# Strassen's seven products for twenty pairs of column blocks of the gate and up projections, and the SiLU product split into high and low parts in the down projection

## The chip, the cores and the metric

The kernel runs on one core of a Trainium2 chip. The metric is the device time of one execution in microseconds; the time before is the median of three runs. A core has a matrix engine (TensorE, in the profile PE for matmuls and PEld for the loads of their stationary operand), a vector engine (VectorE, DVE), a scalar engine (ScalarE, ACT), GpSimd (POOL), and SyncE (SP), which here issues the weight loads. Each engine works through its own queue in order and waits on semaphores for the others. TensorE writes its results to PSUM, in tiles of two halves of 512 float32 columns; everything else is in SBUF.

## The reference, cut to what matters

One layer of a hybrid encoder for 512 prompt tokens and 128 sample tokens (640 rows, `T`), 1024 features, float32. Three gated branches (a recurrence, a convolution, attention into a memory) are merged and projected, and a feed forward follows:

```python
def trunk_layer(x, ...):
    z = x @ w_in
    ...
    merged = g[:, :, 0] * out_a + g[:, :, 1] * out_b + g[:, :, 2] * out_c
    x = layer_norm(DEEPNORM_ALPHA * x + merged @ w_out, ln1_g, ln1_b)
    ffn = (jax.nn.silu(x @ w_ffn_gate) * (x @ w_ffn_up)) @ w_ffn_down
    x = layer_norm(DEEPNORM_ALPHA * x + ffn, ln2_g, ln2_b)
    return x, ...
```

`w_ffn_gate` and `w_ffn_up` are 1024 x 2816, `w_ffn_down` is 2816 x 1024. The change is in the line that makes `ffn`.

## The kernel before

**Three passes.** A float32 product is made of three matmuls in a faster format (float32r): each operand is split into a high part (a copy by ScalarE into float32r) and a low part (VectorE subtracts the copy from the original), and high x high, high x low and low x high are added up in PSUM. Every operand of these matmuls has to be split first, weights too.

**Tiling.** The activations of the feed forward lie feature-major in `xh` and `xl`: eight blocks of 128 features by 640 tokens. The columns of gate and up come in 22 blocks of 128 (`KF`). One column block is one step (`x_step`, line 696): for each of the eight blocks of features, three passes over two halves of the tokens (`HT`, 320), 48 matmuls into a PSUM tile `pu`, of which there are two. What follows (`evac`, line 1481) is done for gate by ScalarE, which writes SiLU of the result into a slot, and for up by VectorE, which multiplies the slot by the result; then the product is split at once into two slots, `hT[m]`, for the down projection. Slots are 48 SBUF buffers of 640 float32 columns, handed out in turn (`s_` and numbers in the rows).

**Steps and preparation.** The program is a list of `Step`s, written out by the loop at line 1623. A step has a weight (part of a `Load`), a generator of matmuls and an `evac`. At step i the loop first has ScalarE copy the weights of step i+2 (`prep_hi`, into `wh`, three buffers), runs the step's `before`, then issues the matmuls; at the generator's first pause it lets pending streams go on (`advance`), does the `evac` of step i-1 (`flush`), and has VectorE write the low part of the weights of step i+2 (`prep_lo`, into `wl`, three buffers). Weights come in 1 MB loads of 256 columns by SP into two buffers `wr`; a load is issued when all users of the one two before have been split (`Load.take`, `pump`).

**The start and end of the feed forward.** The first three steps (blocks 0 and 1 of gate, 0 of up) form a group: their first token halves run while the norm of the last tokens is still being made. Then come block 1 of up and the other 40 blocks, gate pair and up pair in turn. The down projection (line 1549) takes token tiles 0, 1, 2 first, 22 steps of 18 matmuls of 512 columns with `hT[k]` as the stationary operand, then tiles 3 and 4. `before_down` (line 1496) starts the loads of the residual rows.

Of the kernel before, what the change touches and what calls it, by code (L numbers as in the profile page):

```python
# [20 lines left out]
HT = T // 2  # L21
# [30 lines left out]

class Engine:
    """an engine whose instructions add to an estimate of the time until which it is busy"""
# [89 lines left out]
def trunk(ctx, tc, x_prompt, x_sample, mem_prompt, state_conv_a, state_lru, state_conv_b, cache_mem_k, cache_mem_v,  # L144
# [75 lines left out]
    class Blocks:  # L220
        """two blocks of rows of a weight, in slots"""
# [8 lines left out]
    class Row:  # L230
        """a block of rows of a weight, in slots"""
# [21 lines left out]
    class Step:  # L253
        """weights (a part of a load, in two parts), products (a generator that pauses within), what follows"""

        def __init__(self, ld, part, shape, mm, evac=None, before=None, eng=V, slot=False, wait=False, now=False):
            self.ld, self.part, self.shape, self.mm, self.evac = ld, part, shape, mm, evac
            self.before = before
# [4 lines left out]
        def prep_hi(self):  # L263
# [3 lines left out]
            if self.slot:  # L267
# [4 lines left out]
                self.todo = [(hi[c], lo[c], src[c]) for c in range(2)]  # L272
            else:
# [9 lines left out]
        def prep_lo(self):  # L283
# [5 lines left out]
            self.ld.take()  # L289

# [12 lines left out]
    def advance():  # L303
        """lets the streams go on, as far as the vector and scalar engines have time for them while TensorE is busy"""
# [18 lines left out]
    def until(cond):  # L323
        """goes on with the streams, in turn, until a condition holds"""
# [38 lines left out]
    # ---------------------------------------------------------------- constants  # L363
# [22 lines left out]
    # ---------------------------------------------------------------- early loads  # L386
# [55 lines left out]
    def ln_scale(y, mv, rs):  # L442
        """rows without their mean, over their deviation, on ScalarE"""
# [20 lines left out]
    def to_xt(t, x):  # L464
        """transposes of a token tile into xh/xl columns"""
# [137 lines left out]
    def load_rows():  # L603
        """parameters and states, as rows"""
# [45 lines left out]
    def lambda_rows():  # L650
        """8 * log_sigmoid(lambda)"""
# [17 lines left out]
    # ---------------------------------------------------------------- feature-major products  # L669
# [26 lines left out]
    def x_step(ld, o, evac, group=None):  # L696
        """128 columns of a weight, times xh/xl; in a group the first half of the tokens goes first"""
# [26 lines left out]
    # order of the weight loads and the steps -------------------------------------------------  # L724
    # glu and q
# [43 lines left out]
    # ---------------------------------------------------------------- branch B: convolution, layer norm, swish  # L769
# [49 lines left out]
    def token_row(cols):  # L819
        """[128, 5] per-token values (tokens on partitions) -> [128, 640] rows on every partition, in PSUM"""  # L820
# [5 lines left out]
    def ln_b_stream():  # L826
# [32 lines left out]
        # a hundred columns, where one would do: with fewer TensorE's clock goes down  # L859
# [59 lines left out]
    def block(p, i):  # L919
        """a quarter of a PSUM tile"""  # L920
        return p[:, i // 2, (i % 2) * 256:(i % 2 + 1) * 256]

    def attn_prompt():
# [35 lines left out]
        def queries(_):  # L959
            # queries of the samples in float32: of the even ones, of the odd ones, and zeros for the others  # L960
# [69 lines left out]
    def every(x, e):  # L1030
        """the columns of the even samples or of the odd ones"""
        return x.rearrange("p (j e t) -> p j e t", e=2, t=TS)[:, :, e]

    def attn_sample():
        """A pair of samples has 32 columns of the array and 32 partitions of the results to itself; the odd one's
        products add to zeros on the even one's rows, and the other way round."""
# [3 lines left out]
        def load(to, src, h):  # L1040
            """a head's keys or values, memory rows on partitions"""
# [100 lines left out]
    # ---------------------------------------------------------------- gates and projections  # L1142
# [60 lines left out]
    # ---------------------------------------------------------------- branch A: convolution, recurrence  # L1203
# [28 lines left out]
    def lru_stream():  # L1232
# [79 lines left out]
        # states  # L1312
# [41 lines left out]
    # ---------------------------------------------------------------- step list of the first part  # L1354
# [15 lines left out]
    # ---------------------------------------------------------------- output projection, layer norm 1  # L1370
# [4 lines left out]
    def tm(p, l, w, t, first, last, cs=(0, 1)):  # L1375
        """a token tile's products with a row of blocks of a weight"""
# [297 lines left out]
```

## Time and profile before

| | |
|---|---|
| median of three runs | 1127.92 us (1127.79 to 1129.1) |
| profiled execution | span 1129.4 us; no separate time of it is listed |
| TensorE busy | 1100.2 us (97%), 7115 matmuls |
| VectorE, ScalarE, GpSimd busy | 53%, 37%, 15% of the span |
| feed forward up to the down projection | about 658 to 969.6 us of the span |
| down projection | from 969.6 us |
| granted TensorE clock, mean | 0.993 |

The span runs from the first to the last instruction. All instructions of the five engines are issued through one helper, so rows carry line L64; they are told apart by what they write and read (`pu<-xh,wh` is a matmul of the weight's high part and the activation's high part into a tile `pu`; `s` is any slot). In the chain of waits and in the timelines the first two columns are the start and the length in us, and `[a <-B]` says how long the engine sat idle and what released it. In rows of instruction groups stand the shapes, the count, busy time in us, mean ns of one, and the idle time before. In windows each engine has its busy time and count, then come the granted clock, the DMA share and GB/s.

### The profile page before, as it was taken

What the parts mean: (1) busy time and instruction counts of PE and PEld (TensorE: products, weight loads), DVE (VectorE), ACT (ScalarE), POOL (GpSimd) and SP (SyncE); (2) the same over time, 40 slices, a digit from 0 to 9 for tenths busy, and PEclk for the clock granted to TensorE, in tenths of its full rate; (3) what the DMA queues carried; (4) which work ended last, traced back from release to release, by engine and by line L of the source; (5) the groups of instructions that cost most, each with busy time, mean ns of one, the idle gap of its engine ahead of it and who ended that gap; (6) DMA issues with size and microseconds to landing.
All of it is one profiled execution on the core that took longest, in us unless ns stands there. A gap on an engine that the chain in (4) does not pass through costs nothing.

```text
span 1129.4 us, 16818 instructions
## 1 busy us (share of the span) xinstructions
PE 1100.2 (97%) x7115; PEld 1047.0 (93%) x7115; DVE 595.5 (53%) x895; ACT 420.7 (37%) x635; POOL 170.5 (15%) x185
## 2 busy tenths in 40 slices
PE   8799998989999999999999999999999999999997
PEld 7699998979999999999998899999999999888886
DVE  6929988992465665571354763222222222322675
ACT  3532554435446556862222122222222222222341
POOL 3623333646000000010001310000000000100111
PEclk9999999999999999999999999999999999999998
DMA  9632113624122222222227223222222222634481
GB/s 340 226 102 75 38 50 113 197 81 138 53 92 75 74 77 75 75 80 75 75 76 242 93 76 112 75 75 75 75 75 75 75 75 76 234 121 133 153 292 38
DMA packets 80331, 123.11 MB, mean 109 GB/s; under 512 B 4075, under 2 KB 59371, under 8 KB 80256
## 3 DMA queue, kind: packets, MB, share of 16 engines
q1 hardware_dynamic: 73168, 100.36, 27.2%
q0 software_dynamic: 7088, 21.68, 6.1%
q8 instruction: 56, 0.92, 0.3%
q14 instruction: 19, 0.16, 0.0%
HBM read 112.41 MB, written 9.61 MB: 108 GB/s over the span
## 4 chain that ended last, share of the span: by engine, by line
PE 78%; DVE 12%; ACT 4%; issue 2%; DMA 2%; POOL 1%; SPq 0%; DVEq 0%; POOLq 0%
PE pu L64 69%; DVE s L64 10%; PE pv L64 9%; ACT s L64 2%; DVE wl L64 1%; ACT L64 1%; DMA wr<-in_w_in 1%; ACT wh L64 1%; DMA s<-in_w_mem_k 0%; DMA s<-in_w_mem_v 0%; DMA s<-in_ln_in_g 0%; POOL s L516 0%; DVE xres L64 0%; POOL s L517 0%; POOL rs L439 0%
## 5 line engine op out<-in xcount | busy, mean ns | idle before, releaser
L64 PE MATMUL pu<-xh,wh 128*128 128x320 f32 x1504 | 351.4, 311 | 2.1 <-DVE s L64 1.5
L64 PE MATMUL pu<-xl,wh 128*128 128x320 f32 x1504 | 348.5, 309 | 0.0
L64 PE MATMUL pu<-xh,wl 128*128 128x320 f32 x1504 | 348.3, 309 | 0.0
L64 ACT ACTIVATE wh<-wr 128x1024 fp32r<-128x1024 f32 (+1 forms) x161 | 163.6, 1017 | 494.4 <-PE pu L64 273.4
L64 DVE TENSOR_TENSOR wl<-wr,wh 128x1024 fp32r<-128x1024 f32 (+1 forms) x148 | 173.0, 1169 | 275.5 <-ACT wh L64 275.3
L64 PEld LDWEIGHTS pu<-xh,wh 128*128 128x128 f32 x1504 | 252.3, 188 | 5.5 <-issue 2.0
L64 PEld LDWEIGHTS pu<-xl,wh 128*128 128x128 f32 x1504 | 253.3, 188 | 0.6 <-DVE xl L64 0.6
L64 PEld LDWEIGHTS pu<-xh,wl 128*128 128x128 f32 x1504 | 253.3, 188 | 0.0
L64 DVE SCALAR_TENSOR_TENSOR s<-s,pb,s 128x511 f32<-128x511 f32 (+14 forms) x240 | 128.5, 608 | 4.8 <-ACT s L64 4.8
L64 PE MATMUL pu<-wh,s 128*128 128x512 f32 (+1 forms) x396 | 116.5, 386 | 0.0
L64 DVE TENSOR_TENSOR s<-s,s 128x640 f32<-128x640 f32 (+3 forms) x116 | 85.7, 758 | 47.2 <-ACT s L64 43.6
L64 DVE TENSOR_TENSOR s<-s,pu 128x640 f32<-128x640 f32 x48 | 39.3, 819 | 131.7 <-PE pu L64 131.7
L64 PE MATMUL pu<-s,wh 128*128 128x320 f32 x512 | 96.2, 310 | 1.1 <-DVE s L64 0.9
L64 PEld LDWEIGHTS pu<-wh,s 128*128 128x128 f32 x396 | 73.2, 190 | 14.9 <-DVE s L64 0.4
L64 PEld LDWEIGHTS pu<-s,wh 128*128 128x128 f32 x512 | 80.2, 188 | 1.9 <-DVE s L64 1.5
L64 ACT ACTIVATE s<-s 128x640 fp32r<-128x640 f32 (+3 forms) x100 | 64.1, 663 | 32.3 <-DVE s L64 31.3
L64 PE MATMUL pu<-wl,s 128*128 128x512 f32 (+1 forms) x198 | 62.8, 389 | 1.5 <-POOL wl L287 0.8
L287 POOL TENSOR_TENSOR wl<-wr,wh 128x1024 fp32r<-128x1024 f32 x13 | 48.2, 3711 | 96.3 <-ACT wh L64 90.2
L64 PE MATMUL pu<-s,wl 128*128 128x320 f32 x256 | 58.3, 309 | 0.0
L64 PE MATMUL pv<-wh,s 128*128 128x512 f32 (+1 forms) x152 | 48.7, 367 | 0.3 <-DVE xres L64 0.3
L1499 POOL DMA_DIRECT2D xres<-x x5 | 2.6, 535 | 305.6 <-PE pu L64 305.6
L64 PEld LDWEIGHTS pu<-wl,s 128*128 128x128 f32 x198 | 37.4, 191 | 10.5 <-POOL wl L287 1.7
(126 smaller groups left out, 929.4 us busy)
## 6 DMA issues: line engine op xcount, KB each, us to landing
wr<-in_w_in SPq DMA_DIRECT2D x26, 1024.0 KB, 5.7
wr<-in_w_ffn_down SPq DMA_DIRECT2D x19, 1024.0 KB, 5.7
wr<-in_w_ffn_gate SPq DMA_DIRECT2D x11, 1024.0 KB, 5.4
wr<-in_w_ffn_up SPq DMA_DIRECT2D x11, 1024.0 KB, 5.3
s<-in_cache_mem_k POOLq DMA_DIRECT2D x16, 256.0 KB, 7.6
s<-in_cache_mem_v POOLq DMA_DIRECT2D x16, 256.0 KB, 6.8
wr<-in_proj_a SPq DMA_DIRECT2D x4, 1024.0 KB
wr<-in_w_out SPq DMA_DIRECT2D x4, 1024.0 KB, 5.1
```

Of the source, the lines that this page charges most:

```text
L64: return f(*a, **k)
L287: self.eng.tensor_tensor(l, x, f32(h), op=OP.subtract)
L1499: G.dma_start(r[:, t], scratch["x1"][t * 128:(t + 1) * 128, :])
```

## The change

Block columns 0 and 1 of gate and up stay as they were, except that the product of SiLU and up stays whole, in one slot. Blocks 2 to 21 are taken in ten pairs for gate and ten for up. A pair is a 2 x 2 problem: two halves of the tokens (320 each) by two halves of the features (four blocks each), times two halves of the features by two column blocks. Winograd's form of Strassen's scheme makes it of seven products in place of eight. For that

- four sums of quarters of the activations, s1 to s4, are made once and split (`sums_stream`, a stream started when block 0 of gate is done; it has to be finished before the second product of the first pair),
- four sums of quarters of each weight tile, t1 to t4, are made by VectorE in slots (`sums_1`, `sums_2`), in the third and fourth step of the pair before,
- each product is a `Step` of its own with 12 matmuls of 320 columns. The high and low parts of its weight share one buffer, alternately of `wh` and `wl`. Products m2, m7 and m3 add onto m1, m6 and m5, in the PSUM half where those lie, after they have been read,
- the results are combined by VectorE (`after`, `put`), and SiLU and the product with it are done 320 columns at a time.

The split of the SiLU product moves: `before_down` splits blocks 0 and 1, and each of the first 20 steps of the down projection splits the block two ahead. Docstrings and comments are dropped throughout.

```diff
@@ class Step
-        def __init__(self, ld, part, shape, mm, evac=None, before=None, eng=V, slot=False, wait=False, now=False):
+        def __init__(self, ld, part, shape, mm, evac=None, before=None, eng=V, slot=False, wait=False, now=False,
+                     half=None, after=None):
...
+            elif self.half is not None:
+                n = ("wh", "wl")[self.half]
+                both = view(wp.tile([128, 1024], F32R, name=n, tag=n), [128, 2, *self.shape[1:]])
+                hi, lo = both[:, 0], both[:, 1]
+                self.todo = [(hi, lo, src)]
...
             self.ld.take()
+            if self.after:
+                self.after()
@@ feed forward
+                    hT[m] = get([128, T])
+                    A.activation(c2(hT[m]), p, AF.Silu)
+                    if m == 0:
+                        stream("sums", sums_stream())
+                else:
+                    V.tensor_mul(c2(hT[m]), c2(hT[m]), p)
...
+    def sums_stream():
+        parts = {n: ([], []) for n in ("s1", "s2", "s3", "s4")}
+        for i in range(0, half, 2):
+            a = {}
+            for n, (t0, k0) in {"21": (HT, 0), "22": (HT, half), "11": (0, 0), "12": (0, half)}.items():
+                a[n] = get([128, 2, HT])
+                V.tensor_tensor(a[n], *(f32(x[:, k0 + i:k0 + i + 2, t0:t0 + HT]) for x in (xh, xl)), op=OP.add)
+                yield "v"
+            s = {}
+            for n, p, q, op in (("s1", "21", "22", OP.add), ("s2", "s1", "11", OP.subtract),
+                                ("s3", "11", "21", OP.subtract), ("s4", "12", "s2", OP.subtract)):
+                s[n] = get([128, 2, HT])
+                V.tensor_tensor(s[n], s[p] if p in s else a[p], s[q] if q in s else a[q], op=op)
+                yield "v"
+            free(*a.values())
+            for n, x in s.items():
+                hi, lo = get([128, 2, HT], F32R), get([128, 2, HT], F32R)
+                split(hi, lo, x)
...
+        def sums_1(self):
+            self.add("t3", "22", "12", OP.subtract)
+            self.add("t2", "t3", "11", OP.add)
+
+        def sums_2(self):
+            self.add("t1", "12", "11", OP.subtract)
+            self.add("t4", "t2", "21", OP.subtract)
...
+    PRODUCTS = (("m1", 0, 0, True, "11", "11"), ("m6", 0, 1, True, "s2", "t2"), ("m2", 0, 0, False, "12", "21"),
+                ("m7", 0, 1, False, "s3", "t3"), ("m5", 1, 0, True, "s1", "t1"), ("m4", 1, 1, True, "22", "t4"),
+                ("m3", 1, 0, False, "s4", "22"))
...
+        def after(n, p):
+            if n == "m1":
+                tmp["a"], tmp["b"] = get([128, 2, HT]), get([128, 2, HT])
+                copy(tmp["a"][:, 0], p)
+            elif n == "m6":
+                V.tensor_tensor(tmp["a"][:, 1], tmp["a"][:, 0], p, op=OP.add)
+            elif n == "m2":
+                put(0, 0, p, None, None)
+            elif n == "m7":
+                V.tensor_tensor(tmp["b"][:, 0], tmp["a"][:, 0], p, op=OP.add)
+            elif n == "m5":
+                put(1, 1, p, tmp["b"][:, 0], OP.add)
+            elif n == "m4":
+                put(0, 1, p, tmp["b"][:, 0], OP.subtract)
...
+            else:
+                put(1, 0, p, tmp["a"][:, 1], OP.add)
...
+                for k in range(half):
+                    P.matmul(p, hi[:, k], xhi[k], start=start and k == 0, stop=False, skip_group_check=not start)
+                    P.matmul(p, hi[:, k], xlo[k], start=False, stop=False, skip_group_check=not start)
+                yield
+                for k in range(half):
+                    P.matmul(p, lo[:, k], xhi[k], start=False, stop=k == half - 1, skip_group_check=not start)
+                yield
...
+            if i == 1:
+                before = begin
+            elif following and i == 2:
+                before = following.sums_1
+            elif following and i == 3:
+                before = following.sums_2
...
+    last_of_first = steps[-2]
+    last_of_first.before = lambda: (pairs[0][0].sums_1(), pairs[0][0].sums_2())
...
+        def put(j, c, p, x, op, which=which, m2=m2):
+            if which == "g":
...
+                h = c2(hT[m2 + j])[:, c]
+                if x is not None:
+                    V.tensor_tensor(h, x, p, op=op)
+                A.activation(h, p if x is None else h, AF.Silu)
+            else:
+                h = c2(hT[m2 + j])[:, c]
+                if x is not None:
+                    y = get([128, HT])
+                    V.tensor_tensor(y, x, p, op=op)
+                    V.tensor_tensor(h, h, y, op=OP.mult)
+                    free(y)
+                else:
+                    V.tensor_tensor(h, h, p, op=OP.mult)
...
+    def split_h(k):
+        if k < KF:
+            hi, lo = get([128, T], F32R), get([128, T], F32R)
+            split(hi, lo, hT[k])
...
     def before_down():
+        flush()
+        free(*sums)
+        for k in range(2):
+            split_h(k)
...
                 wd[k] = halves(w)
+                if len(tiles) == 3:
+                    split_h(k + 2)
```

**How it moves instructions.** TensorE, within the feed forward. Before, from a step of one column block (both token halves each time, hence x2):

```order
L64 MATMUL pu<-xh,wh 128x320 x2
L64 MATMUL pu<-xl,wh 128x320 x2
L64 MATMUL pu<-xh,wl 128x320 x2
L64 MATMUL pu<-xh,wh 128x320 x2
L64 MATMUL pu<-xl,wh 128x320 x2
```

After, the second product of the first pair, m6, and the first row of m2. Here `wl` is a buffer with both parts of t2, `s_370` and `s_388` are the high parts of s2, `s_371` and `s_389` its low parts:

```order
L64 MATMUL pu<-s_370_6712,wl 128x320
L64 MATMUL pu<-s_371_6713,wl 128x320
L64 MATMUL pu<-s_370_6712,wl 128x320
L64 MATMUL pu<-s_371_6713,wl 128x320
L64 MATMUL pu<-s_388_6766,wl 128x320
L64 MATMUL pu<-s_389_6767,wl 128x320
L64 MATMUL pu<-s_388_6766,wl 128x320
L64 MATMUL pu<-s_389_6767,wl 128x320
L64 MATMUL pu<-s_370_6712,wl 128x320 x2
L64 MATMUL pu<-s_388_6766,wl 128x320 x2
L64 MATMUL pu<-xh,wh 128x320
```

A product is 12 matmuls into one half of a PSUM tile, and m6 reads both halves of s2, of which the second is made last.

VectorE, where the feed forward begins, behind the last split of the normed activations (`xl<-pv,xh`). Before, with the low parts of weights (`wl<-wr,wh`), the products with SiLU and their splits:

```order
L64 TENSOR_TENSOR xl<-pv,xh 128x4x128 x4
L64 TENSOR_TENSOR wl<-wr,wh 128x1024 x2
L64 TENSOR_TENSOR s_354_6585<-s_354_6585,pv 128x640
L64 TENSOR_TENSOR s_357_6662<-s_354_6585,s_356_6661 128x640
L64 TENSOR_TENSOR wl<-wr,wh 128x1024
L64 TENSOR_TENSOR s_355_6617<-s_355_6617,pu 128x640
```

After, the end of the same stretch: the second half of the sums of activations, from the whole quarters (`<-xh,xl`) over s1 to s4 (`s_382` to `s_385`) to their low parts (`s_387` to `s_393`):

```order
L64 TENSOR_TENSOR s_381_6752<-xh,xl 128x640
L64 TENSOR_TENSOR s_382_6754<-s_378_6746,s_379_6748 128x640
L64 TENSOR_TENSOR s_383_6756<-s_382_6754,s_380_6750 128x640
L64 TENSOR_TENSOR s_384_6758<-s_380_6750,s_378_6746 128x640
L64 TENSOR_TENSOR s_385_6760<-s_381_6752,s_383_6756 128x640
L64 TENSOR_TENSOR s_387_6763<-s_382_6754,s_386_6762 128x640
L64 TENSOR_TENSOR s_389_6767<-s_383_6756,s_388_6766 128x640
L64 TENSOR_TENSOR s_391_6771<-s_384_6758,s_390_6770 128x640
L64 TENSOR_TENSOR s_393_6775<-s_385_6760,s_392_6774 128x640
L64 TENSOR_TENSOR wl<-s_358_6610,wl 128x512
L64 TENSOR_TENSOR s_394_6793<-wr 128x512
L64 TENSOR_TENSOR s_395_6795<-s_394_6793,wr 128x512
```

Behind the low part of the weight of up's block 1 stand 23 instructions of 640 columns and 7 of 512 ahead of the one that writes `s_389`, the last part of s2; the two splits of SiLU products that stood there are gone.

VectorE, where the down projection begins. Before, the product for block 21 of up (`s_415`), its split, and 22 low parts of weights:

```order
L64 TENSOR_TENSOR s_414_8848<-s_414_8848,pu 128x640
L64 TENSOR_TENSOR s_417_8962<-s_414_8848,s_416_8961 128x640
L64 TENSOR_TENSOR wl<-wr,wh 128x1024
L64 TENSOR_TENSOR s_415_8905<-s_415_8905,pu 128x640
L64 TENSOR_TENSOR s_419_9015<-s_415_8905,s_418_9014 128x640
L64 TENSOR_TENSOR wl<-wr,wh 128x1024 x22
```

After, from the reading of the last product (`s_557`) on:

```order
L64 TENSOR_TENSOR s_557_9383<-s_553_9281,pu 128x320
L64 TENSOR_TENSOR s_552_9228<-s_552_9228,s_557_9383 128x320
L64 TENSOR_TENSOR s_559_9387<-s_354_6585,s_558_9386 128x640
L64 TENSOR_TENSOR s_561_9391<-s_362_6630,s_560_9390 128x640
L64 TENSOR_TENSOR s_563_9404<-s_398_6825,s_562_9403 128x640
L64 TENSOR_TENSOR wl<-wr,wh 128x1024
```

The low part of the first SiLU block, `s_559`, with which the down projection's first step works, now stands behind the reading of the last product.

More of the change, by code (lines that the diff above doesn't have):

```diff
@@ new lines, in trunk, with evac @@
+    for which in ("g", "u"):
+        for m in range(2):
+            def evac(p, m=m, which=which):
+                if which == "g":
[5 more added lines that the diff above has]
+                    V.tensor_mul(c2(hT[m]), c2(hT[m]), p)
+            x_step(zload[which], m * 128, evac, group=group if len(group[1]) < 3 else None)
+    half = KD // 2
@@ new lines, in trunk @@
+    quarters = {}
+    for n, (t0, k0) in {"11": (0, 0), "12": (0, half), "21": (HT, 0), "22": (HT, half)}.items():
+        quarters[n] = tuple([x[:, k0 + k, t0:t0 + HT] for k in range(half)] for x in (xh, xl))
+    sums = []
+    def sums_stream():
[16 more added lines that the diff above has]
+                split(hi, lo, x)
+                free(x)
+                sums.extend((hi, lo))
+                for to, y in zip(parts[n], (hi, lo)):
+                    to.extend(y[:, k] for k in range(2))
+                yield 1
+        quarters.update(parts)
@@ new lines, in trunk @@
+    pairs = []
+    for m2 in range(2, KF, 2):
+        for which, w in (("g", w_ffn_gate), ("u", w_ffn_up)):
+            pairs.append((Pair(ffn_load(w, m2, 7)), which, m2))
+    last_of_first = steps[-2]
+    last_of_first.before = lambda: (pairs[0][0].sums_1(), pairs[0][0].sums_2())
+    for i, (pair, which, m2) in enumerate(pairs):
+        def put(j, c, p, x, op, which=which, m2=m2):
+            if which == "g":
+                if m2 + j not in hT:
+                    hT[m2 + j] = get([128, T])
+                h = c2(hT[m2 + j])[:, c]
[11 more added lines that the diff above has]
+                    V.tensor_tensor(h, h, p, op=OP.mult)
+        seven(pair, put, pairs[i + 1][0] if i + 1 < len(pairs) else None,
+              begin=(lambda: finish("sums")) if i == 0 else None)
```

59 lines of the change are left out of this document (41 added, 18 removed).

## The prediction

> **What bounds the kernel now.** I read the page's engine row first, then the chain that ended last in order of time, then the feed forward stage by windows.
>
> ```profile
> span 1129.4 us, 16818 instructions
> PE 1100.2 (97%) x7115; PEld 1047.0 (93%) x7115; DVE 595.5 (53%) x895; ACT 420.7 (37%) x635; POOL 170.5 (15%) x185
> ```
>
> TensorE is busy 97% of the span, VectorE 53%, ScalarE 37%. A busy share is an average over stages, so the chain has to say where TensorE ends last:
>
> ```profile
> 667.01 3.52 PE pv L64 x24
> 670.53 7.04 PE pu L64 x48
> 677.58 3.52 PE pv L64 x24
> 681.10 291.38 PE pu L64 x1980
> 972.48 1.36 PE pv L64 x6
> ```
>
> From 681.10 on the chain is TensorE alone for 291.4 us. Those 1980 matmuls are 41 steps of 48 of the feed forward and, at the end, the first 12 of the down projection (512 wide, 1.36/6 = 0.227 us each). So (291.38 - 12 x 0.227)/1968 = 0.1467 us per 320-wide matmul, 7.04 us per column block. The row at 677.58 gives the same for 24 matmuls into one half of one PSUM tile: 3.52/24 = 0.1467. Neither a step's border nor repeated writes into one half cost anything.
>
> ```profile
> 681.00:972.00 291.00, 291.00 (x1980) 290.59 (x1979) 84.37 (x85) 72.64 (x84) 1.73 (x4) 1.00 0.25 77
> PE pv L64 <- DVE xres L64: 0.3, 1, 0.3
> ```
>
> The first row (windows: PE, PEld, DVE, ACT, POOL busy, granted clock, DMA share, GB/s) says that VectorE works 84 of these 291 us and ScalarE 73, at a granted clock of 1.00. The second is TensorE's whole list of waits from 655 us to the end. The stage is bound by the number of matmuls, and the helpers have some 200 us to spare.
>
> **Matmuls removed.** Two column blocks cost 2 x 48 = 96 matmuls. As a pair they cost seven products of four blocks of rows and three passes, 84, all 320 wide; the order lists 5232 of that width for 5472 before and the same number of every other width. So 240 go: 240 x 0.1467 = **-35.2 us**. The new passes read the same weights twice running (high part times high, high times low) as before, into one half of a tile, which the row at 677.58 prices. The rule in the Trainium skill, "TensorE: Matmul & The Clock Gate", section "Back-to-back issue gap", makes a warm gap columns/2.4 + 2.5 ns, 135.8 ns for 320; by it the term would be -32.6 and the whole sum -22.7. The trace's 146.7 is what these matmuls take, and I use it.
>
> **Prices of the helpers' work.** Rows of the instruction groups by form, and of VectorE's and ScalarE's timelines:
>
> ```profile
> L64 DVE TENSOR_TENSOR wl<-wr,wh 128x1024 fp32r<-128x1024 f32 x43 | 52.6, 1222 | 105.7 <-ACT wh L64 105.7
> L64 DVE TENSOR_TENSOR s<-s,s 128x640 fp32r<-128x640 f32 x21 | 17.3, 826 | 16.9 <-ACT s L64 16.9
> L64 DVE TENSOR_TENSOR s<-s,pu 128x640 f32<-128x640 f32 x20 | 16.4, 821 | 84.2 <-PE pu L64 84.2
> L64 DVE TENSOR_TENSOR xl<-pv,xh 128x512 fp32r<-128x512 f32 x4 | 2.6, 685 | 0.3 <-ACT xh L64 0.3
> L64 ACT ACTIVATE wh<-wr 128x1024 fp32r<-128x1024 f32 x42 | 44.6, 1062 | 217.3 <-issue 107.6 <-PE pu L64 104.1 <-PE pv L64 5.6
> L64 ACT ACTIVATE s<-s 128x640 fp32r<-128x640 f32 x20 | 14.8, 740 | 0.7
> ```
>
> ```profile
> 666.41 1.29 DVE L64 TENSOR_TENSOR xl<-pv,xh 128x512 fp32r<-128x512 f32 x2 [0.26 <-ACT xh L64]
> 675.04 1.23 DVE L64 TENSOR_TENSOR wl<-wr,wh 128x1024 fp32r<-128x1024 f32 x1 [7.34 <-ACT wh L64]
> 689.80 0.83 DVE L64 TENSOR_TENSOR s<-s,s 128x640 fp32r<-128x640 f32 x1 [0.81 <-ACT s L64]
> 690.54 1.22 DVE L64 TENSOR_TENSOR wl<-wr,wh 128x1024 fp32r<-128x1024 f32 x1
> ```
>
> Instructions on VectorE overlap a little: after one of 640 columns the next starts 0.74 us later (689.80 to 690.54), and its result is there 0.09 later still (0.83). For 512: 1.29 - 0.685 = 0.605. The line through these two, 1.05 ns a column, gives 0.40 for 320 columns, which the trace doesn't have, and 1.14 for 1024. Reading PSUM costs no more than reading slots (821 against 826). An instruction that needs the one just before it loses 0.09.
>
> **The ten pairs in steady state.** Per pair VectorE splits seven weights of 512 columns (7 x 0.605), makes four weight sums (4 x 0.605) and adds or multiplies results 320 wide, five times for gate and nine times for up. That is 6.7 + 2.0 = 8.7 us and 6.7 + 3.6 + 0.4 for dependent ones = 10.7 us, against 84 x 0.1467 = 12.3 us of matmuls. ScalarE has seven copies of 512 columns and up to five of 320; even at the full 0.74 of the 640 row that is 8.9. Both fit, in order too. A product is a slot of 1.76 us. Two places are tight, both because a product adds onto a bank that must first be read: m7 needs m6 read within m2's slot, m3 needs m5 read within m4's. In m2's slot VectorE has the next pair's first two sums ahead of that read: 2 x 0.605 + 0.09 + 0.40 = 1.7, under 1.76 even if it starts them only then, and it is free to start them in m6's slot. Weights are prepared two slots ahead, 3.5 us, for at most 2.4 us of work. I put this at nothing; if the cover goes, it costs what the third rival says.
>
> The sums also wait for the weight's load, now held by seven steps.
>
> ```profile
> wr<-in_w_ffn_gate SPq DMA_DIRECT2D x11, 1024.0 KB, 5.4
> 652.44 0.37 SPq L247 DMA_DIRECT2D wr<-in_w_ffn_gate  x1
> 676.29 0.37 SPq L247 DMA_DIRECT2D wr<-in_w_ffn_up  x1
> ```
>
> SP issues a load when the seventh split of the pair two before is done, in the fifth slot (about 8 us into a pair of 12.3); it lands 5.4 us later, 1 to 1.5 us into the next pair, and its first sum stands in the second or third slot, from 1.8 us on. Nothing waits. The first pair's two loads go out at 652.44 and 676.29 as before, long before they are read.
>
> **The opening: a new wait.** The second product, m6, needs s2, a sum of quarters of the activations. The order shows what VectorE has between the last split that the trace shows there (675.04, free for the next at 676.18) and s2's last low part: 24 instructions of 640 columns and 7 of 512, three of them dependent. 24 x 0.74 + 7 x 0.605 + 3 x 0.09 = 22.3, so 698.5 with the result's delay. TensorE without it would come to m6 after the first four column blocks and m1: 681.10 + 7.04 + 1.76 = 689.9. It issues five matmuls of m6, waits until 698.5, does the other seven (1.03) and m2 (1.76) and is at m7 at 701.3. There it waits for m6 to be read, which stands behind two instructions of 640, three of 512 and its own 320: 698.5 + 1.48 + 1.8 + 0.5 = 702.3. Undisturbed, m7 would start at 689.9 + 2 x 1.76 = 693.4. The term is **+8.9 us**. Everything behind m6 in TensorE's queue waits with it; nobody else is hurt, since ScalarE's copies of the second half of the sums stand behind m1's copy but are done about 696.4 for s2.
>
> Bounds: 0 if all hid, and 11.5 if every instruction took its full duration (24 x 0.83 + 7 x 0.685 = 24.7 in place of 22.3, and as much delay again in proportion behind it). I keep 8.9.
>
> **The clock in that gap.** Windows of the kernel's tail:
>
> ```profile
> 1121.00:1122.00 1.00, 0.26 (x3) 0.05 (x1) 0.67 (x2) 0.00 (x0) 0.14 (x1) 1.00 0.00 0
> 1123.00:1124.00 1.00, 0.00 (x0) 0.00 (x0) 1.00 (x3) 0.00 (x0) 0.73 (x1) 0.68 0.00 0
> 1124.00:1125.00 1.00, 0.00 (x0) 0.00 (x0) 1.00 (x2) 0.00 (x0) 0.00 (x0) 0.50 0.00 0
> ```
>
> The last matmul ends at 1121.26; the granted clock (behind the five engines) is 0.50 by 1124 and, from the mean of 0.68, halved at about 1123.4, 2.1 us after. The opening's gap has 6 us without a matmul, so m6 resumes at half clock. No row shows how long that lasts. TensorE then has 1.0 us to give away before m7, so 2.0 us at half clock cost nothing: zero in the sum, the rest is a rival.
>
> **The down projection's start.** The first two halves of the SiLU product are split only when the last product's result has been combined.
>
> ```profile
> 969.57 0.63 PE L64 MATMUL pu<-wh,s 128*128 128x512 f32 x2
> 969.77 0.82 DVE L64 TENSOR_TENSOR s<-s,pu 128x640 f32<-128x640 f32 x1 [3.45 <-PE pu L64]
> ```
>
> Before, the down projection starts at 969.57 while VectorE, from 969.77, reads the last result, so a result is read 0.2 us after its step. Now VectorE adds (0.40), multiplies (0.09 + 0.40) and writes the low part (0.83): 1.9 us after the step. TensorE's fifth matmul needs it at 4 x 0.227 = 0.9 us. **+1.0 us**. The copy on ScalarE that it starts with waits for nothing of the last product. The bounds are 0 and 1.9. The other 20 splits stand two blocks of rows ahead: with the weight's, 0.74 + 1.14 on VectorE and at most 0.74 + 1.06 on ScalarE against 18 x 0.227 = 4.1 us. Nothing.
>
> **Sum.** -35.2 + 8.9 + 1.0 = -25.3 us. The profiled execution's span, 1129.4, would become 1104.1. Its own time isn't listed beside the span; the median of the three runs is 1127.92, 1.5 below that span, and I carry the difference over: **1102.6 us**.
>
> **Rivals.**
>
> *The clock stays halved.* If it takes two or three times the 2.1 us that it took to fall, m6, m2 and m7 run at half clock for 4.2 to 6.3 us; half of it, less the 1.0 to spare, is +1.1 to +2.2: 1103.7 to 1104.8. For it: the tail's 0.50. Against: no row, since the trace never shows the clock come back. Chance 0.20. The same page of the Trainium skill, section "What's actually happening", speaks against this change here: it has the clock halved after some 3.4 us of idleness and given back only after some 3.4 us of work, an estimate of +0.7 us in this sum. The tail agrees with the fall, which came sooner.
>
> *The opening costs less.* If VectorE's adds are shorter or s2 is read later than I think, up to 8.9 more is saved, 1093.7 at the least. Chance 0.05.
>
> *VectorE falls behind in each pair.* In up pairs it has 10.7 of 12.3 us. If waits for TensorE cost it a slot's rest here and there, m7 or m3 waits; 0.3 to 0.5 us in each of 20 pairs is 6 to 10 us: 1108.6 to 1112.6. For it: VectorE at 71% to 87% in strict order with waits in each slot. Against: the places above leave a slot's time or more. Chance 0.15.
>
> *Slower than before: TensorE can't write one half of a PSUM tile while the other half is read.* Before, a result is read while TensorE writes another tile; now six or seven reads of a pair fall on a tile whose other half is being written, some 0.4 to 0.5 us each, 3 us a pair. If all of it stops TensorE, 20 x 3 = 60 us are added, and the time is 1102.6 + 60 = 1163. It decides from 25.3/20 = 1.27 us a pair, two fifths of the reading time. For it: no row before shows the two together. Against: TensorE's first rows of m2, in the order, carry no wait for the read of m6. Chance 0.06.
>
> *It doesn't do what it says.* The new products could run their matmuls at a wider spacing, since each is only 12 long: 25.3/1680 = 15 ns more a matmul and nothing is left, 1127.9. Against: the rows above, with short runs at 0.1467. Chance 0.02.
>
> **How the numbers follow.** The forecast alone has 0.52, with a range of its own of 1100.5 to 1105. Low end 1099.5: VectorE's 24 adds each 0.1 us shorter, and a little. High end 1111.5, which takes in the clock and nearly all of the lag in each pair. Outside are the slower case, no change and most of the cheap opening, about 0.12. A measurement of this kernel tells 0.2% (2.3 us) from no change. Faster by more: 0.52 + 0.20 + 0.05 + 0.15 = 0.92; within 0.02; slower 0.06.
>
> **What would show it.** In the profile after: 240 matmuls fewer, and the same 0.147 us each in the pairs; in TensorE's waits one for VectorE of some 6 us and one of some 2 us between 688 and 703, a third of about 1 us where the down projection starts, and none else; VectorE's busy share of the pairs near 80%. The prediction is wrong if waits of TensorE for VectorE or ScalarE recur in every pair, if a pair takes clearly more than 12.3 us, or if the opening's gap is under 5 or over 12 us.

## The result, and the profile after

The changed kernel takes 1190.79 us (median of four runs, 1188.28 to 1192.51) against 1128.04 for the kernel before (four runs, 1127.79 to 1129.1): the ratio is 1.0552, 95% interval 1.0535 to 1.057. That is 62.8 us slower, where I had forecast 25.3 us faster, and far outside the range.

The page of the changed kernel, its span and its engine row:

```profile
span 1190.7 us, 16903 instructions
PE 1097.9 (92%) x6875; PEld 1015.9 (85%) x6875; DVE 750.0 (63%) x1219; ACT 473.3 (40%) x783; POOL 166.5 (14%) x185
```

The 240 matmuls are gone (7115 to 6875), yet TensorE's share falls from 97% to 92%. VectorE is far from full. Next, the windows of two successive stretches of the feed forward, a gate and an up pair each, and TensorE's whole list of waits from 726 to 1026 us (sum, count, longest):

```profile
726.63:759.72 33.09, 27.31 (x168) 24.68 (x168) 20.25 (x37) 10.34 (x20) 0.00 (x0) 1.00 0.21 65
759.72:792.81 33.09, 27.31 (x168) 24.69 (x168) 20.26 (x37) 10.34 (x20) 0.00 (x0) 1.00 0.21 65
```

```profile
PE pu L64 <- DVE s L64: 38.4, 64, 0.7
PE pu L64 <- ACT s L64: 14.2, 27, 0.5
```

Two pairs take 33.09 us, to the hundredth each time, at a granted clock of 1.00: 16.55 us a pair, where 84 x 0.1467 = 12.32 was forecast. The list has 91 waits in 299 us, or 18 pairs: **five a pair**, each at most 0.7 us. In the kernel before, the list had none in that stage. The timelines show what such a wait is. First TensorE from the end of m6 to m7 of an up pair (start, length, operation, count, idle time before and its releaser), then VectorE over the same time:

```profile
783.17 0.85 PE L64 MATMUL pu<-s,wh 128*128 128x320 f32 x4 [0.53 <-ACT s L64]
...
784.89 0.31 PE L64 MATMUL pu<-xl,wl 128*128 128x320 f32 x1
785.85 0.85 PE L64 MATMUL pu<-xh,wl 128*128 128x320 f32 x4 [0.65 <-DVE s L64]
786.54 1.33 PE L64 MATMUL pu<-s,wh 128*128 128x320 f32 x8
788.45 0.85 PE L64 MATMUL pu<-s,wh 128*128 128x320 f32 x4 [0.58 <-DVE s L64]
```

```profile
785.31 0.49 DVE L64 TENSOR_TENSOR s<-s,pu 128x320 f32<-128x320 f32 x1 [1.99 <-PE pu L64]
785.71 0.69 DVE L64 TENSOR_TENSOR wl<-s,wl 128x512 fp32r<-128x512 f32 x1
...
787.91 0.49 DVE L64 TENSOR_TENSOR s<-s,pu 128x320 f32<-128x320 f32 x1 [0.32 <-PE pu L64]
```

m6 ended at 783.17 + 0.85 = 784.02. VectorE has nothing to do, and still it starts to read m6 only at 785.31, right behind the eighth matmul of m2 (784.89 + 0.31 = 785.20). Then TensorE's other four matmuls of m2 wait for that read (785.31 + 0.49 = 785.80) and start at 785.85. But m6 lies in one half of the tile and m2 in the other; neither touches the other's data. So it goes at m1's read in m6 (783.17, released by ScalarE), m6's in m2 (785.85), m2's in m7 (788.45), m5's in m4 and m4's in m3, and not at m7's in m5, where two successive products lie in different tiles. One break costs the 0.53 to 0.65 us of waiting, the time for the eighth matmul to run out, and about 0.1 us more for the first four behind it (0.69 in place of 0.587): 4.22 / 5 = 0.84 us.

The rest of the difference lies at the two ends of the stage. The opening, TensorE's timeline and windows of the granted clock (behind the five engines):

```profile
686.10 0.31 PE L64 MATMUL pu<-xh,wh 128*128 128x320 f32 x1
...
688.55 0.85 PE L64 MATMUL pu<-s,wl 128*128 128x320 f32 x4 [0.53 <-ACT s L64]
694.49 0.64 PE L64 MATMUL pu<-s,wl 128*128 128x320 f32 x1 [5.09 <-ACT s L64]
696.67 2.23 PE L64 MATMUL pu<-s,wl 128*128 128x320 f32 x7 [1.54 <-DVE s L64]
...
706.39 1.92 PE L64 MATMUL pu<-s,wh 128*128 128x320 f32 x12
```

```profile
702.00:704.00 2.00, 2.00 (x9) 2.00 (x9) 1.97 (x4) 0.00 (x0) 0.00 (x0) 0.50 0.00 0
704.00:706.00 2.00, 1.47 (x7) 1.07 (x6) 0.00 (x0) 0.78 (x2) 0.00 (x0) 0.68 0.00 0
```

From m1 (686.10) to m5 (706.39) pass 20.3 us, where four products are 7.0: 13.3 us late. The account below counts three of the breaks in there (2.5 us), which leaves 10.7 for the opening. That is a remainder and not a measured term: the break ahead of m6 (688.55) falls into a stop that is there anyway, and the clock, still halved behind the break in m2, slows the first eight matmuls of m7 as well. And the down projection's start, in TensorE's timeline, the chain of waits and a window:

```profile
1027.10 0.86 PE L64 MATMUL pu<-s,wl 128*128 128x320 f32 x4 [0.58 <-DVE s L64]
1028.88 0.73 PE L64 MATMUL pu<-wh,s 128*128 128x512 f32 x2 [0.92 <-ACT s L64]
```

```profile
1028.88 4.81 PE pu L64 x12
1033.69 1.36 PE pv L64 x6
1035.05 2.72 PE pu L64 x12
```

```profile
1030.00:1032.00 2.00, 2.00 (x5) 1.29 (x5) 2.00 (x4) 0.09 (x1) 0.00 (x0) 0.50 0.99 395
```

Before, the second step of the down projection stood at 973.84 in the chain, 4.27 us behind the last product of the stage (969.57); now it stands at 1035.05, 7.26 us behind it (1027.10 + 4 x 0.172 = 1027.79): 3.0 us, a stop and then twelve matmuls in 4.81 us, at half the clock for the most part. The account is -35.2 (matmuls) + 20 x 4.22 = 84.4 (breaks) + 10.7 (opening) + 3.0 (down projection) = +62.9, against 62.8 between the medians. The agreement to a tenth is luck: between the two profiled executions the difference is 61.3 us (1190.7 - 1129.4), and the one of the changed kernel comes to m1 2.0 us earlier (686.10 in place of 681.10 + 7.04 = 688.14), which lies ahead of the pairs.

### The profile page after: what moved, and what is told of

It reads as the page before. It is cut to its first block, busy times and chain, and to the rows that moved or that the text cites. A ratio compares the mean times of both kernels' runs of the same rounds, so it can differ in the third digit from the quotient of the medians.

```text
span 1190.7 us, 16903 instructions
## 1 busy us (share of the span) xinstructions
PE 1097.9 (92%) x6875; PEld 1015.9 (85%) x6875; DVE 750.0 (63%) x1219; ACT 473.3 (40%) x783; POOL 166.5 (14%) x185
## 4 chain that ended last, share of the span: by engine, by line
PE 75%; DVE 13%; ACT 5%; issue 3%; DMA 2%; POOL 1%; SPq 0%; DVEq 0%; POOLq 0%; ACTq 0%
PE pu L64 66%; DVE s L64 12%; PE pv L64 9%; ACT s L64 3%; DVE wl L64 1%; DMA s<-in_x_sample 1%; ACT L64 1%; ACT wh L64 1%; DMA s<-in_mem_prompt 1%; DMA s<-in_w_mem_v 0%; DMA s<-in_ln_in_b 0%; POOL s L524 0%; DVE xres L64 0%; POOL s L525 0%; DMA s<-in_b_gate 0%
## 5 line engine op out<-in xcount | busy, mean ns | idle before, releaser
L64 PE MATMUL pu<-xh,wh 128*128 128x320 f32 x1104 | 267.1, 315 | 14.3 <-DVE s L64 13.7
L64 PE MATMUL pu<-xh,wl 128*128 128x320 f32 x1104 | 262.7, 311 | 12.3 <-DVE s L64 12.3
L64 PE MATMUL pu<-xl,wh 128*128 128x320 f32 x984 | 239.1, 310 | 0.0
L64 PE MATMUL pu<-s,wh 128*128 128x320 f32 x992 | 181.0, 312 | 17.9 <-DVE s L64 12.5
L64 DVE TENSOR_TENSOR s<-s,pu 128x320 f32<-128x320 f32 (+1 forms) x138 | 76.5, 554 | 168.9 <-PE pu L64 168.9
L64 PEld LDWEIGHTS pu<-xl,wh 128*128 128x128 f32 x984 | 169.5, 189 | 0.6 <-DVE xl L64 0.6
L64 PE MATMUL pu<-s,wl 128*128 128x320 f32 x736 | 145.8, 317 | 23.0 <-ACT s L64 15.6
L64 DVE TENSOR_TENSOR s<-s,s 128x640 f32<-128x640 f32 (+4 forms) x162 | 112.3, 714 | 72.6 <-ACT s L64 67.9
L64 PEld LDWEIGHTS pu<-s,wl 128*128 128x128 f32 x736 | 117.0, 191 | 31.6 <-ACT s L64 21.3
L64 ACT ACTIVATE s<-s 128x640 fp32r<-128x640 f32 (+4 forms) x138 | 83.6, 623 | 93.8 <-DVE s L64 93.3
```

What stands on the lines that cost most here:

```text
L64: return f(*a, **k)
```

## The experiments

**Theory.** The waits that the program carries are kept for a PSUM tile as a whole. A product's read is issued in the middle of the next product, behind eight of its matmuls into the other half, so it is made to wait for those eight, and the four behind it are made to wait for the read. **Rival 1:** TensorE itself cannot write while the bank beside it is read. **Rival 2:** VectorE and ScalarE fall behind in their strict order.

**Two tiles.** The halves become tiles of their own; nothing else changes.

```diff
-                if start and c == 0:
-                    acc[u] = pu()
-                p = acc[u][:, c, :HT]
+                if start:
+                    acc[u, c] = pu() if c == 0 else ps.tile([128, 2, 512], F32, name="pv", tag="v", bufs=2)
+                p = acc[u, c][:, c, :HT]
```

> The two halves of each accumulator of the Strassen pairs become two PSUM tiles (first half in a pu tile, second half in a pv tile); every product, read and sum stays, and the banks a read and a write touch at one time are still two different ones. Theory 1 (waits are kept per whole PSUM tile: the read of one half is made to wait for the matmuls already issued into the other half, and the next four matmuls for the read): the five breaks of about 0.85 us a pair go, a pair takes 12.3 to 12.6 us in place of 16.55, 20 x 4.2 = 84 us come back, 1104 to 1110 us. Rival 1 (TensorE cannot write while another engine reads the bank beside it, whatever the program's waits): the breaks stay, 1180 to 1195 us. Rival 2 (VectorE and ScalarE fall behind in strict order): most of the breaks stay as waits at other places, 1150 us or more.

Measured: 1107.54 us, ratio to the kernel before 0.9821 (0.9807 to 0.9834). The chain of waits in the pairs is TensorE alone, and its whole list of waits from 660 to 1060 us has four entries: two in the opening, one where the down projection starts, one later in the down projection, and none in a later pair. The row of windows is as long as one pair:

```profile
706.82 3.52 PE pu L64 x24
710.34 1.76 PE pv L64 x12
...
719.14 3.52 PE pu L64 x24
```

```profile
PE pv L64 <- ACT s L64: 5.9, 1, 5.9
PE pu L64 <- ACT s L64: 2.7, 1, 2.7
PE pv L64 <- DVE s L64: 1.5, 1, 1.5
PE pv L64 <- DVE xres L64: 0.4, 1, 0.4
```

```profile
717.22:729.54 12.32, 12.32 (x87) 12.32 (x85) 10.63 (x19) 3.58 (x7) 0.00 (x0) 1.00 0.28 86
```

A pair takes 719.14 - 706.82 = 12.32 us, as forecast. And TensorE writes one tile at its full rate while the other is read. TensorE's rows, then VectorE's:

```profile
705.05 0.31 PE L64 MATMUL pv<-xl,wl 128*128 128x320 f32 x1
705.19 0.31 PE L64 MATMUL pv<-xh,wl 128*128 128x320 f32 x1
```

```profile
705.10 0.49 DVE L64 TENSOR_TENSOR s<-s,pu 128x320 f32<-128x320 f32 x1 [0.67 <-PE pu L64]
```

The read at 705.10 runs while matmuls start every 0.147 us. The waits in the two programs say the rest. In the changed kernel the read of m6 waits for TensorE's count as it stands behind the eighth matmul of m2, which writes the other half, and the ninth matmul waits for VectorE's count as it stands behind that read. With two tiles the read waits for m6 alone, and the first matmul that waits for it is the first of m7, which adds onto m6. So the theory holds, and rival 2 falls. Of rival 1 it falls that a read of PSUM as such stops TensorE. Whether TensorE could write one half of a tile while the other half of the same tile is read is not shown: in the changed kernel the waits keep the two apart, and with two tiles the halves in use belong to different tiles. The breaks need no such limit. The Trainium skill, "PSUM — Partial Sum Buffer", section "Summary: rules for kernel authors", says that a read during matmuls should go to another bank than theirs, and that banks are what is to be guarded. A half of 512 float32 columns is one such bank by that page's terms. The run agrees that this much is enough (0 us of waiting); the changed kernel's waits were coarser than that.

**Another order, one tile.** The products alternate between the two tiles: m1, m4, m6, m5, m7, m2, m3, so that only m7's read falls on a tile that is being written. m4 and m5 are combined behind m7; m5 is copied out first.

```diff
+    PRODUCTS = (("m1", 0, 0, True, "11", "11"), ("m4", 1, 1, True, "22", "t4"), ("m6", 0, 1, True, "s2", "t2"),
+                ("m5", 1, 0, True, "s1", "t1"), ("m7", 0, 1, False, "s3", "t3"), ("m2", 0, 0, False, "12", "21"),
+                ("m3", 1, 0, False, "s4", "22"))
...
+            elif n == "m5":
+                copy(tmp["b"][:, 1], p)
```

> One tile for both halves, as in the changed kernel, but the seven products go in the order m1, m4, m6, m5, m7, m2, m3, so that the product that runs while another is read lies in the other tile, but for the read of m7 in m2. m5 is copied out by ScalarE for that, one more copy of 320 columns a pair. Theory 1: one break of 0.85 us a pair is left of five: 12.32 + 0.85 = 13.2 us a pair, and the first product that needs a sum comes one product later, which saves up to 1.8 us once: 1119 to 1125 us. Rival 1 (reads of PSUM themselves stop TensorE): one read more a pair than before, so no gain, 1185 us or more. Rival 2 (VectorE behind): the helpers' work is the same or a little more, so little gain, 1160 us or more.

Measured: 1130.16 us, ratio 1.0013 (1.0004 to 1.0022): 60 us of the loss come back by the order alone, but the time is 5 us over what I gave. Two pairs take 27.09 us, 24.64 + 2.45. TensorE's timeline:

```profile
746.28 0.85 PE L64 MATMUL pu<-xh,wh 128*128 128x320 f32 x4 [0.58 <-DVE s L64]
746.98 1.93 PE L64 MATMUL pu<-s,wl 128*128 128x320 f32 x12
749.42 0.38 PE L64 MATMUL pu<-xh,wh 128*128 128x320 f32 x1 [0.52 <-DVE s L64]
```

The first row is the one break that I expected. The third I had missed: behind an up pair the next m1 goes into the tile of m2, whose read stands at the end of five operations of VectorE behind m7. Two breaks and that wait, 2 x 0.84 + 0.76, are the 2.45. So the theory holds in its count, and the miss is a wait that the new order made.

**The read right behind its product**, ahead of the next one, tiles and order unchanged.

```diff
-                 half=parity[0] % 2, after=lambda wn=wn: pair.drop(wn))
+                 half=parity[0] % 2, now=True, after=lambda wn=wn: pair.drop(wn))
```

> The changed kernel with each product's read issued right behind its last matmul, ahead of the next product, in place of behind the next product's eighth matmul; tiles and order of products unchanged. Theory 1: the same five reads a pair fall between writes of the same tile, now at the product's end, so five breaks of 0.7 to 0.9 us a pair stay: 1183 to 1196 us. Rival 2 (VectorE behind, reads too late): reads come earlier by eight matmuls, 1.2 us each, and most of the loss goes, under 1150 us.

Measured: 1192.46 us, ratio 1.0573 (1.0558 to 1.0587). TensorE's waits from 726 to 1026 us:

```profile
PE pu L64 <- DVE s L64: 40.7, 63, 0.7
PE pu L64 <- ACT s L64: 14.2, 27, 0.5
```

90 waits in place of 91, as long as before. The read no longer waits for foreign matmuls, but the next product, in the same tile, now waits for the read from its first matmul. The two places of the read cost the same; what they have in common is the shared tile.

**The split in the down projection alone**, on the kernel before.

```diff
-                        hi, lo = get([128, T], F32R), get([128, T], F32R)
-                        split(hi, lo, s)
-                        free(s)
-                        hT[m] = (hi, lo)
+                        hT[m] = s
...
+        for k in range(2):
+            split_h(k)
```

> The kernel before, all products plain, with only the split of the SiLU product moved into the down projection as in the changed kernel. My prediction's term: +1.0 us (0 to 1.9), 1128 to 1130 us. Rival: as the changed kernel's trace has it at that place, a stop of 1.2 us and then half the granted clock for some 3 us, +3.3 us, 1131 to 1132 us.

Measured: 1130.22 us, ratio 1.0018 (1.0009 to 1.0027), 2.0 us more than before, between the two. ScalarE's timeline at the start of the down projection, TensorE's, and the chain of waits:

```profile
967.70 1.06 ACT L64 ACTIVATE wh<-wr 128x1024 fp32r<-128x1024 f32 x1 [5.98 <-PE pu L64]
968.66 1.98 ACT L64 ACTIVATE s<-s 128x640 fp32r<-128x640 f32 x3
```

```profile
969.44 0.73 PE L64 MATMUL pu<-wh,s 128*128 128x512 f32 x2 [1.48 <-ACT s L64]
```

```profile
969.44 3.02 PE pu L64 x12
```

The stop of 1.48 us and a first twelve matmuls of 3.02 us (2.72 before) make 1.8. TensorE waits for the high part, the second row of ScalarE. That copy needs nothing of the last product, but it stands behind the copy of a weight for a later step, and that one waits until TensorE has left a buffer.

**The early split**, on two tiles: the first two halves of the SiLU product are split in the last pair.

```diff
+            elif not following and i in (2, 3):
+                before = lambda i=i: split_h(i - 2)
```

> Two tiles, and the first two halves of the SiLU product are split during the last pair's third and fourth product in place of in front of the down projection. In the run with two tiles TensorE stands 2.74 us there, since the copy of the SiLU product on ScalarE stands behind the copy of a weight of the down projection whose load lands late. Theory: that stop goes, 1107.5 - 2.7 = 1104.8 us (1103.8 to 1106). Rival: the weight's load itself is what TensorE waits for, and the stop only moves some 4 us further on: 1107 us or more.

Measured: 1104.53 us, ratio 0.9785 (0.9771 to 0.9798), as expected; the wait of 2.7 us is gone and no other came.

**A plain gate pair first**, on two tiles: blocks 2 and 3 of gate as plain column blocks, 19 pairs.

```diff
+    ld2 = ffn_load(w_ffn_gate, 2, 2)
+    for m in (2, 3):
...
+        x_step(ld2, (m - 2) * 128, evac)
...
-        for which, w in (("g", w_ffn_gate), ("u", w_ffn_up)):
+        for which, w in (("g", w_ffn_gate), ("u", w_ffn_up))[m2 == 2:]:
```

> Two tiles, and the first gate pair is made of two plain column blocks again (19 pairs in place of 20), so that VectorE has 14.1 us more for the sums of the activations before the first product that needs one. Cost: one pair's saving, 12 matmuls, +1.76 us. Theory: the opening's stop and the half clock behind it go, which in the run with two tiles put the fourth product at 701.55 in place of 690.9, 10.65 us late: 1107.5 - 10.65 + 1.76 = 1098.6 us (1097.5 to 1100). Rival: VectorE needs the time anyway and a wait comes at a later product: 1102 us or more.

Measured: 1098.47 us, ratio 0.9732 (0.9719 to 0.9746). The opening's waits are gone, and none came later but that of the down projection (2.5 us).

**Both**, the fastest version:

> Two tiles, the first gate pair plain and the early split, together. If the terms add: 1107.5 - 8.9 - 2.7 = 1095.9 us (1094.5 to 1097.5). If they share a cause, more.

Measured: 1094.93 us, ratio to the kernel before 0.9699 (0.9686 to 0.9712): the terms add. TensorE's whole list of waits from 660 to 1060 us, and the row of windows of the stage:

```profile
PE pv L64 <- DVE xres L64: 0.4, 1, 0.4
```

```profile
678.79:932.23 253.44, 253.44 (x1731) 253.44 (x1730) 210.34 (x365) 108.51 (x203) 0.00 (x0) 1.00 0.26 81
```

TensorE is busy without a pause. 19 pairs save 19 x 12 x 0.1467 = 33.4 us, and 1128.4 - 33.4 = 1095.0.

**The clock in the opening**, on two tiles: 28 idle matmuls ahead of m6.

```diff
+                if warm and n == "m6":
+                    q = ps.tile([128, 2, 512], F32, name="pv", tag="v", bufs=2)
+                    for z in range(28):
+                        P.matmul(q[:, 0, :128], ident, ident, start=True, stop=True)
```

> Two tiles, with 28 idle matmuls of the unit matrix (128 wide, about 0.21 us each, 5.9 us) put ahead of the second product, in the stop where TensorE waits for the sum; nothing else is changed. They keep TensorE busy, so the clock should not fall. Theory: the 19 matmuls from the resumption to the fourth product take 2.8 us in place of 5.36, of which 1.0 to 2.6 us reaches the end, since the fourth product may then wait for the second to be read: 1105 to 1106.5 us. Rival: the clock falls by something else than idleness and nothing changes: 1107.5 us.

Measured: 1107.17 us, one run. The granted clock stays at 1.00 in the whole opening. m5 starts 16.23 us behind m1 (685.52 to 701.75) where it was 17.52 with two tiles alone (685.62 to 703.14), so 1.29 us are won, and m7 then waits 0.75 us for m6's read, as in my prediction. But the end shows nothing of it. The start of the down projection in this run, in TensorE's timeline, the chain of waits and a window:

```profile
943.92 1.22 PE L64 MATMUL pu<-wh,s 128*128 128x512 f32 x2 [2.65 <-ACT s L64]
```

```profile
943.92 4.44 PE pu L64 x12
```

```profile
944.00:946.00 2.00, 2.00 (x5) 1.62 (x6) 2.00 (x3) 1.12 (x2) 0.00 (x0) 0.50 0.99 379
```

With two tiles alone a stop of 2.74 us stands there, the clock stays at 1.00 behind it, and the first twelve matmuls take 3.04 us: 2.74 + 0.32 = 3.1 us late. Here the clock is halved behind the stop: 2.65 + 1.72 = 4.4 us late. So the price of the clock in the opening is shown at its place, 1.3 us in one run; that it carries to the end is not.

## Why the prediction was wrong

**The step that failed** is "The ten pairs in steady state", which I put at nothing. It measured 20 x 4.22 = 84.4 us. Its prices were right: an operation of 320 columns frees VectorE after 0.40 us (785.31 to 785.71), as forecast, and with two tiles VectorE's work fits into the pair, 10.63 of 12.32 us in the row of windows above. What failed is the rule by which I let a read start. I asked only whether a bank is read before a later product adds onto it (the two tight places, m7 and m3). I took a read and a write of two halves for independent in the program, and never asked what its waits take them for. Without this step's loss the sum would nearly have stood: with two tiles the result is 1107.54, 4.9 over the forecast and inside the range.

**The rival that came closest** is the one that I gave 0.06, a stop while the other half is read, with 3 us a pair and 1163 us. Place and number of stops were right (five in place of six or seven). Its cause, a limit of TensorE itself, is not what stops it: the waits stand in the program, and they go with the shared tile. Its price was low, since a stop holds not just the read (0.49 us) but also the run-out of the eighth matmul before it and the refill behind it, 0.84 together. What I held against it, that the first rows of m2 carry no wait for m6's read, was true and no argument. The order of TensorE's instructions in m2 of the first pair:

```
2742 L64 MATMUL pu<-xh,wh 128x320
...
2749 L64 MATMUL pu<-xl,wh 128x320
2750 L64 MATMUL pu<-xh,wh 128x320 [waits DVE_49]
2751 L64 MATMUL pu<-xh,wh 128x320 x3
```

The wait stands at the ninth row. I took it for the wait for the low part of the weight, which begins to be used there and is VectorE's too. The row names only the engine. That the low part had been written two products earlier should have made me ask which instruction of VectorE is the last one ahead of that row: it is the read.

**Matmuls removed, -35.2.** Right: 84 matmuls at 0.1467 are 12.32, and a pair on two tiles takes 12.32. By the gap of the Trainium skill, "TensorE: Matmul & The Clock Gate", section "Back-to-back issue gap", which I had weighed there, it would be 84 x 0.1358 = 11.4, an estimate that no run bears out.

**The opening, +8.9.** Right but for the clock: on two tiles m5 is 17.52 - 7.04 = 10.5 us late, 9.2 of it with the clock held up and 1.3 by the clock. TensorE resumed at 696.67 in the changed kernel; my 698.5, moved with VectorE's last undisturbed split (673.17 for 675.04), is 696.6.

**The clock, 0 in the sum.** Wrong by 1.3 us at the place; the rival that gave it 1.1 to 2.2 was right about the size. That the trace before never shows the clock come back was a wrong reading: it does, at two places in the first 260 us. At the second of them the last matmul ends at 246.04 and TensorE resumes at 251.02. Windows of the kernel before:

```profile
249.00:250.00 1.00, 0.00 (x0) 0.00 (x0) 1.00 (x3) 0.00 (x0) 0.56 (x1) 0.77 0.00 0
256.00:257.00 1.00, 1.00 (x7) 1.00 (x7) 1.00 (x4) 1.00 (x3) 0.00 (x0) 0.82 0.13 41
```

From these means the clock halves at about 249.5 and is back at about 256.4, 5.3 us after TensorE resumed. Half of that, less the 1.0 us to spare, is 1.7, an estimate that I could have put into the sum.

**The down projection's start, +1.0.** Too low: 1.8 us in the trace of the split alone, 3.0 in the changed kernel, 3.1 on two tiles. I followed VectorE's low part; the high part on ScalarE was later, behind the copy of a weight in the same queue. "The copy on ScalarE that it starts with waits for nothing of the last product" named the wrong thing to look for: it is not what that copy reads, but what stands ahead of it. On two tiles it is a copy that waits for a load:

```profile
943.67 1.06 ACT L64 ACTIVATE wh<-wr 128x1024 fp32r<-128x1024 f32 x1 [5.19 <-DMA wr<-in_w_ffn_down]
944.63 1.98 ACT L64 ACTIVATE s<-s 128x640 fp32r<-128x640 f32 x3
```

In the changed kernel TensorE stops 0.9 us there, and the first step runs in part at half clock.

**VectorE falls behind in each pair,** 0.15: it did not happen; on two tiles no wait of a pair is left.

## What to carry to other kernels

Where a change lets one engine read a part of a buffer while another writes a different part, find out at what grain the program's waits are kept, and give the parts buffers of their own if they are kept for the whole; in the trace such a wait shows as an idle reader that starts exactly when a foreign write ends. A wait in the order says which engine is waited for, not for what: look for the last instruction of that engine ahead of it. And a short copy is as late as whatever stands ahead of it in its engine's queue.

## What the runs showed of the hardware

The granted clock comes back late. In the opening on two tiles the last matmul ahead of the stop has ended at 687.38 + 0.75 = 688.13. The clock, worked out from the mean of its microsecond, halves at about 691.1. TensorE resumes at 696.19, works without a pause, and has the full clock only at about 701.3, 5.1 us later. In the changed kernel, with a break of 0.58 us in between, it is 8.6 us (696.67 to about 705.3). TensorE's timeline on two tiles, and windows:

```profile
687.38 0.75 PE L64 MATMUL pv<-s,wl 128*128 128x320 f32 x4
...
696.19 2.23 PE L64 MATMUL pv<-s,wl 128*128 128x320 f32 x7 [1.54 <-DVE s L64]
```

```profile
691.00:692.00 1.00, 0.00 (x0) 0.00 (x0) 1.00 (x2) 0.00 (x0) 0.00 (x0) 0.53 0.00 0
701.00:702.00 1.00, 1.00 (x8) 1.00 (x7) 1.00 (x3) 0.42 (x2) 0.00 (x0) 0.84 0.00 0
```

The Trainium skill, "TensorE: Matmul & The Clock Gate", section "What's actually happening", has both changes after about 3.4 us, in a window that runs freely and so lands differently from run to run. Here the fall took 2.1 us in the kernel before's tail, 2.9 in this opening and 3.5 at 249.5 in the kernel before, and the return without a break 5.1 and 5.3; whether the landing alone makes these differences no run here tells. Two more things fit some such window. A stop of 2.7 us ahead of the down projection halved the clock in the run with idle matmuls and not in the one without. And the breaks of 0.6 us, five a pair, left the clock at 1.00 in all of the pairs, while at the down projection two of them and a stop of 0.9 us close together were followed by half of it.
